# Weights 64 bytes and rests 192 bytes aside, and three groups of 512-column products made in two halves of 256

## The chip, the cores and the metric

The kernel runs on one core of a Trainium2 chip. The metric is the device time of one execution in microseconds; the runs of the kernel before agree within 0.1%.

## The reference

Two layers of a transformer trunk over 512 tokens of width 1024, all in float32, with a final RMS norm. Cut to what matters:

```
for l in range(2):
    h = rmsnorm(x, attn_norm[l])
    sb_q, sb_k, sb_v, df_q, df_k, df_v = split(h @ w_in[l])     # six parts of 512 columns
    sb_out = stick_breaking_attention(sb_q, sb_k, sb_v)         # 8 heads of 64
    df_out = differential_attention(rope(df_q), rope(df_k), df_v, lam)   # 4 heads, two softmaxes each
    df_out = rmsnorm(df_out, subln_norm[l]) * (1 - lambda_init)
    x = x + concat(sb_out, df_out) @ w_o[l]
    h = rmsnorm(x, mlp_norm[l])
    x = x + square(relu(h @ w_ff1[l])) @ w_ff2[l]               # width 4096
return rmsnorm(x, final_norm)
```

## The kernel before, in words

Every float32 operand is split into two parts that TensorE takes as float32r: `hi`, a rounded copy, and `lo`, the rest. A product of two such pairs is three matmuls into the same PSUM bank, in a fixed order: `three` (line 304) issues hi x hi (L310), hi x lo (L311) and lo x hi (L312). I call the three a triple. The first operand of a matmul is stationary (128 columns, loaded into the array ahead of the product, the PEld rows of the profile); the second is the moving one, 512 or 256 columns here. Within a triple the stationary operand is `ah`, `ah`, `al`, the moving one `bh`, `bl`, `bh`, and each matmul has a load of its own, also where the stationary operand stays the same.

Weights come in units of 128 x 1024 floats. A list of units (`_unit_list`, line 51) fixes their order through both layers. The class `_Weights` loads a unit from HBM into one of three raw tiles and splits it (`split_part`, line 120): ScalarE writes `hi` (L118), VectorE subtracts and writes `lo` (L135). The tiles of the split come from pools in rotation; `whi` has 1024 columns, `wlo` has 1152, of which a unit uses 1024 from a starting column that its kind decides: 16 for "s" units, 48 for "v" units, 0 for all others (`NARROW`, line 40). A column is 4 bytes, so 16 columns are 64 bytes and 48 are 192. All the tiles named here begin at multiples of 256 bytes. The first two "w" units of each layer are split into `md_hi` and `md_lo` instead (`W.home`), which have no starting column.

The kinds of units, with what the products are made of:

- "x": projections of the differential attention's queries and keys; weights stationary, 512 tokens of the normed activations `h_hi`, `h_lo` moving. Made by `block` (line 320).
- "p": projections of the stick-breaking attention's queries and keys, 16 units in both layers together, also by `block`; 8 triples of 512 columns each.
- "w": values of the softmax (differential) attention, 4 units a layer, in `all_values` (line 454): activations stationary, 512 columns of weights moving; 8 triples a unit.
- "v": values of the stick-breaking attention, in `values_of`: activations stationary, weights moving in 256 columns, 128 triples in all.
- "o": output projection, in `wo` (line 795): weights stationary, 512 tokens of the attention's output moving. Half 1 (`md_hi`, `md_lo`) runs among the attention's products, half 0 (`ms_hi`, `ms_lo`, which share their tiles with `vd_hi`, `vd_lo`) after them; 64 triples each in both layers.
- "1", "s", "f": the dense stage. "1" units are the first group's products of 512 columns, by `block`. "s" units are the seven forms of a Strassen-like product of the first dense matrix, weights stationary, activations moving in 256 columns: 7 forms x 8 triples x 2 x 3 groups x 2 layers. "f" units are the forms of the second matrix, weights moving in 512 columns.

Products of 256 columns are not read and written in order: `walked` (line 298) cuts the columns into groups of 32 and takes the groups from the last to the first, for the moving operand and the PSUM bank alike. `three` does this when it is given a `step`; products of 512 columns are taken straight.

In the attention stage the order of TensorE's queue is written out by a planner in the code: `dense` yields after each triple (each six, for "v"), with an assumed cost, and pieces of `attn` (scores S, transposes T, sums O) are put between. The page's names for the outputs are `p0s1k` (layer 0, stick-breaking, block 1, keys), `p0u` ("v" units), `p0w` ("w" units), `wo`, and X, V, Y, W, Z for the dense stage's banks.

Of the kernel before, what the change touches and what calls it, by code (L numbers as in the profile page):

```python
# [10 lines left out]
F32R = mybir.dt.float32r  # L11
# [6 lines left out]
P = 128  # L18
# [4 lines left out]
KC = D // P  # L23
# [13 lines left out]
MAN = ()  # L37
APART = (("s", 0, 1), ("s", 3, 0), ("s", 3, 1))
_CTX = {}
NARROW = {"s": 16, "v": 48}  # L40
DLY_R, DLY_D, DLY_S, DLY_Q = 3.5, 10.2, 9.0, 6.0
TAIL, ATT, DENSE, CAP = 6.0, 53.0, 145.0, 0.1
FORMS = ("11", "x3", "x2", "21", "x1", "x4", "22")
# [9 lines left out]
def _unit_list():  # L53
    units = []
    def qk(l, cq, ck, b):
        units.append(("p", l, cq + b * P))
        units.append(("p", l, ck + b * P))

    for l in range(L):
        for item in ORDER:  # L60
            b = int(item[1])
            if item[0] == "d":
                units.append(("x", l, b, 0))
                units.append(("x", l, b, 1))
            elif item[0] == "s":
                qk(l, SBQ, SBK, b)
            elif item[0] == "w":
                units.extend(("w", l, part) for part in range(4))
            else:
                units.extend(("v", l, SBV + b * P, half) for half in range(2))  # L70
        for half in (1, 0):
            for j in range(4):
                units.append(("o", l, half, j))
        for g in range(GROUPS):
            if g == 0:
                units.extend(("1", l, f) for f in range(2 * GP))
            else:
                units.extend(("s", l, g, j, form) for j in range(2) for form in FORMS)
            for form in FORMS2:
                for c in range(GP // 2):  # L80
                    units.append(("f", l, g, form, c))
    return units


_UNITS = _unit_list()
# [9 lines left out]
class _Weights:  # L95
# [24 lines left out]
    def split_part(self, i, a, b):  # L120
        nc = self.nc
        if i not in self.tiles and i in self.home:
            self.tiles[i] = self.home[i]
        if i not in self.tiles:
            k = self.spot(i)
            self.owner[k] = i
            self.turn = k + 1
            at = NARROW.get(_UNITS[i][0], 0)
            hi = self.pools[k // 2].tile([P, 1024], F32R, tag="whi", name=f"whi{i}")
            lo = self.pools[k // 2].tile([P, 1152], F32R, tag="wlo", name=f"wlo{i}")[:, at : at + 1024]  # L130
            self.tiles[i] = (hi, lo)
        hi, lo = self.tiles[i]
        raw = self.first if (i, b) == (0, P) else self.raw[i]
        h = self.round(hi[:, a:b], raw[:, a:b])
        self.last = h, nc.vector.tensor_tensor(  # L135
            out=lo[:, a:b], in0=raw[:, a:b], in1=hi[:, a:b].bitcast(F32), op=ALU.subtract)
# [31 lines left out]
def trunk(ctx, tc, opened, xT, w, w2, w1, gfin, lamv, cos, sin, out):  # L168
# [11 lines left out]
    def bank(tag, name):  # L180
        if tag == "any":
            tag = ("mm", "s", "s", "mm", "s")[turn[0] % 5]
            turn[0] += 1
        ring[0] += tag == "s"
        return ps.tile([P, 512], F32, tag=tag, name=name, bufs=banks[tag])
# [3 lines left out]
    W = _Weights(nc, w, wraw, wspl)  # L189
# [37 lines left out]
    def gcol(which, l, c):  # L227
        i = {"attn": l * 8, "mlp": 16 + l * 8, "final": 32, "sub": 40 + l}[which] + c
        return g_all[:, i : i + 1]
# [21 lines left out]
    def make_h(c, g):  # L251
        a = nc.scalar.activation(h_hi[:, c, :], x[:, c, :], AF.Copy, scale=g)
        return a, nc.vector.scalar_tensor_tensor(
            out=h_lo[:, c, :], in0=x[:, c, :], scalar=g, in1=h_hi[:, c, :].bitcast(F32),
            op0=ALU.mult, op1=ALU.subtract)

    def add_sq(c, first, sqt, eng=nc.gpsimd):
        if first:
            return nc.scalar.activation(ssq, x[:, c, :], AF.Square), None
        sq = sqt("sq")  # L260
        s = nc.scalar.activation(sq, x[:, c, :], AF.Square)
        return s, eng.tensor_tensor(out=ssq, in0=ssq, in1=sq, op=ALU.add)
# [35 lines left out]
    def walked(t, step):  # L298
        return t.rearrange("p (a b) -> p a b", b=step)[:, ::-1, :]
# [4 lines left out]
    def three(pt, a, b, first, last, goes_on=False, step=0):  # L304
        ah, al = a
        bh, bl = b
        if step:
            pt, bh, bl = (walked(e, step) for e in (pt, bh, bl))
        return (
            nc.tensor.matmul(pt, ah, bh, start=first, stop=False, skip_group_check=goes_on),  # L310
            nc.tensor.matmul(pt, ah, bl, start=False, stop=False, skip_group_check=goes_on),  # L311
            nc.tensor.matmul(pt, al, bh, start=False, stop=last, skip_group_check=goes_on))  # L312

    def hpair(c):
        return h_hi[:, c, :], h_lo[:, c, :]

    def wpair(u, c, n=P):
        return u[0][:, c * n : (c + 1) * n], u[1][:, c * n : (c + 1) * n]

    def block(name, tag="mm"):  # L320
        pt = bank(tag, name)
        u = W.next("px" if name[0] == "p" else "1")
        for c in range(KC):
            three(pt, wpair(u, c), hpair(c), c == 0, c == KC - 1)
            yield pt if c == KC - 1 else None

    def constants(a2):
# [18 lines left out]
    for l in range(L):  # L346
        with ExitStack() as actx:
# [49 lines left out]
            first = W.split  # L397
# [56 lines left out]
            def all_values():  # L454
                pts = [bank(tag, f"p{l}w{tb}") for tb, tag in enumerate(("s", "s", "s", "o"))]
                for part in range(4):
                    u = W.next("w")
                    for n in range(2):
                        c = 2 * part + n
                        wide = wpair(u, n, 512)  # L460
                        for tb, pt in enumerate(pts):
                            h = [e[:, c, tb * P : (tb + 1) * P] for e in (h_hi, h_lo)]
                            W.product = three(pt, h, wide, c == 0, c == KC - 1)[2]
                            if c == KC - 1:
                                hi, lo, r = vd_hi[:, tb, :], vd_lo[:, tb, :], rcol[:, tb : tb + 1]
                                nc.scalar.activation(hi, pt, AF.Copy, scale=r)
                                nc.vector.scalar_tensor_tensor(
                                    out=lo, in0=pt, scalar=r, in1=hi.bitcast(F32), op0=ALU.mult, op1=ALU.subtract)
                            yield
                for i in range(4):  # L470
                    ready[("vd", i)] = clock[0] + 2.5
# [323 lines left out]
            def wo(half):  # L795
                for j in range(4):
                    u = W.next("o")
                    for dd in range(2):
                        db = 2 * j + dd
                        pt = bank("mm" if half else "any", f"wo{l}{half}{db}")  # L800
                        for e in range(4):
                            a = u[0][:, e * 256 + dd * P : e * 256 + dd * P + P]
                            b_ = u[1][:, e * 256 + dd * P : e * 256 + dd * P + P]
                            mh, ml = (md_hi, md_lo) if half else (ms_hi, ms_lo)
                            three(pt, (a, b_), (mh[:, e, :], ml[:, e, :]), e == 0, e == 3)
                            if e < 3:
                                yield 3 * 0.216
                        nc.vector.tensor_add(x[:, db, :], x[:, db, :], pt)
                        if half == 0:
                            ends["h"] = make_h(db, gcol("mlp", l, db))  # L810
                            add_sq(db, db == 0, tt, nc.vector)
                        yield 3 * 0.216

            def dense(pts):
# [24 lines left out]
                for item in ORDER[1:]:  # L839
                    kind, b = item[0], int(item[1])  # L840
                    for which in ("qk" if kind in "ds" else "v"):
# [12 lines left out]
                        if kind in "ds":  # L854
                            {"s": evict_s, "d": evict_d}[kind](pt, kind, b, which)
                yield from wo(1)

            at = attn()
            done = 2 * KC * 3 * 0.216 if l else 0.0
            spent = credit = 0.0  # L860
            live = True
            for cost in dense(pts if l else None):
# [5 lines left out]
                while live and credit > 0:  # L868
                    c = next(at, None)
# [17 lines left out]
        with ExitStack() as fctx:  # L887
# [3 lines left out]
            last = l == L - 1  # L891
# [327 lines left out]
            for g in range(GROUPS):  # L1219
# [24 lines left out]
                for form in FORMS2:  # L1244
# [20 lines left out]
                    for n, (c, i, r, part) in enumerate(work):  # L1265
                        if c not in held:
                            held[c] = W.next("f")
                        u = held[c]
                        hi, lo = (e[:, :, i, :] for e in sides[c])
                        rs = slice(r * P, r * P + P)  # L1270
                        mine = [m for m, e in enumerate(work) if e[2:] == (r, part)]
                        pt, b_ = to[r], wpair(u, i, 512)
                        if part:
                            pt = halves[part - 1][:, 0:256]
                            b_ = [e[:, 256 * part - 256 : 256 * part] for e in b_]
# [8 lines left out]
                        if end and not last and form == "22" and n % 2:  # L1284
                            h = back(n // 2)
# [19 lines left out]
                    if end and last and form == "x1":  # L1305
                        done = ((2, 0), (3, 0), (0, 1), (1, 1))
                        squares = [square(*e) for e in done]
                        weighed = [weigh(*e) for e in done]
                    elif end and last and form == "x4":
                        first = [came[0]]  # L1310
# [5 lines left out]
            else:  # L1316
# [6 lines left out]
                for n in range(KC):  # L1323
                    if n in (3, 5):
                        for c_ in (n + 1, n + 2):
                            h = back(c_)
# [81 lines left out]
```

## Time and profile before

| | us |
|---|---|
| median of 3 runs (1111.13 to 1112.01) | 1111.6 |
| the profiled execution | 1111.63 |
| its span, from the first instruction to the last | 1109.9 |
| PE busy (6345 matmuls) | 1102.4 |
| PEld busy | 964.3 |
| DVE busy | 907.7 |
| ACT busy | 688.6 |

Busy times are sums of recorded durations. PE's recorded matmuls overlap, so the time from one product's start to the next product's start, called a step here, is what a product costs. The rows of a group read: line, engine, operation, output and inputs, shape of the moving operand, count, then busy us and mean ns of one.

### The profile page before, as it was taken

Reading aid. Unit: us, or ns where it says so; the run is one execution under the profiler, and the core shown is the slowest. Engines: PE = TensorE matmul, PEld = TensorE weight load, DVE = VectorE, ACT = ScalarE, POOL = GpSimd, SP = SyncE. Lnnn points to the kernel's source line nnn. Section 1 sums busy time; section 2 is a strip of 40 time slices with the busy share of each in tenths; the row PEclk is TensorE's granted clock in tenths of the full one; section 3 lists DMA queues with packets and bytes.
Section 4 is the critical chain, followed back from the end, with each engine's and each line's share of the span. In section 5 each row is a group of like instructions: output and inputs, shape, how many; then the busy total and the mean of one; then the engine's idle time right before and its main releaser. Section 6 shows DMA issues by size and latency. Waiting matters only on the chain.

```text
span 1109.9 us, 17170 instructions
## 1 busy us (share of the span) xinstructions
PE 1102.4 (99%) x6345; PEld 964.3 (87%) x6345; DVE 907.7 (82%) x1333; ACT 688.6 (62%) x1131; POOL 151.9 (14%) x233
## 2 busy tenths in 40 slices
PE   9999999999999999999999999999999999999997
PEld 7889889888899899899878898888888998998986
DVE  7799688798658879779877897887797787797797
ACT  6447777567558458467345576675774484674765
POOL 1001343101011001001000013530010010010010
PEclk9999999999999999999999999999999999999999
DMA  7476343269777788758325654522577877787462
GB/s 244 146 190 190 112 127 107 83 217 229 185 210 176 179 213 184 191 142 214 110 76 146 189 161 131 161 69 76 208 172 179 210 184 175 203 189 200 123 133 96
DMA packets 61044, 181.25 MB, mean 163 GB/s; under 512 B 7456, under 2 KB 8736, under 8 KB 60960
## 3 DMA queue, kind: packets, MB, share of 16 engines
q1 hardware_dynamic: 50160, 141.84, 40.6%
q0 software_dynamic: 10368, 37.75, 19.8%
q8 instruction: 50, 0.82, 0.3%
q10 hardware_dynamic: 432, 0.56, 0.1%
q14 instruction: 34, 0.28, 0.1%
HBM read 150.77 MB, written 4.19 MB: 140 GB/s over the span
## 4 chain that ended last, share of the span: by engine, by line
PE 97%; DVE 1%; issue 1%; ACT 0%; POOL 0%; POOLq 0%; DVEq 0%; ACTq 0%
PE X L311 9%; PE X L312 9%; PE X L310 9%; PE V L311 4%; PE V L312 4%; PE V L310 3%; PE wo L310 3%; PE wo L312 3%; PE wo L311 3%; PE f L312 3%; PE f L310 3%; PE f L311 3%; PE Y L311 2%; PE Y L312 2%; PE Y L310 2%; PE W L310 1%
## 5 line engine op out<-in xcount | busy, mean ns | idle before, releaser
L118 ACT ACTIVATE whi<-q 128x1024 fp32r<-128x1024 f32 x96 | 101.4, 1057 | 103.9 <-PE X L312 38.1
L135 DVE TENSOR_TENSOR wlo<-q,whi 128x1024 fp32r<-128x1024 f32 x96 | 116.8, 1221 | 42.8 <-ACT whi L118 42.6
L135 DVE TENSOR_TENSOR wlo<-raw,whi 128x1024 fp32r<-128x1024 f32 (+1 forms) x82 | 96.7, 1186 | 6.7 <-ACT whi L118 6.4
L118 ACT ACTIVATE whi<-raw 128x1024 fp32r<-128x1024 f32 (+1 forms) x82 | 80.9, 994 | 33.8 <-issue 17.9
L310 PE MATMUL X<-whi,Ah 128*128 128x512 f32 x248 | 97.4, 393 | 0.0
L312 PE MATMUL X<-whi,Al 128*128 128x512 f32 x248 | 96.7, 390 | 0.0
L311 PE MATMUL X<-wlo,Ah 128*128 128x512 f32 x248 | 96.6, 390 | 0.0
L135 DVE TENSOR_TENSOR wlo<-waves,whi 128x1024 fp32r<-128x1024 f32 x40 | 48.8, 1220 | 15.8 <-ACT whi L118 15.6
L118 ACT ACTIVATE whi<-waves 128x1024 fp32r<-128x1024 f32 x40 | 42.2, 1056 | 29.0 <-PE X L312 18.9
L310 PEld LDWEIGHTS X<-whi,Ah 128*128 128x128 f32 x248 | 46.5, 188 | 11.9 <-DVE y L1132 1.9
L312 PEld LDWEIGHTS X<-whi,Al 128*128 128x128 f32 x248 | 46.5, 188 | 9.8
L311 PEld LDWEIGHTS X<-wlo,Ah 128*128 128x128 f32 x248 | 46.6, 188 | 9.0
L311 PE MATMUL X<-h_lo,whi 128*128 128x256 f32 x192 | 53.6, 279 | 0.0
L311 PE MATMUL X<-hxl,whi 128*128 128x256 f32 x192 | 53.6, 279 | 0.0
L312 PE MATMUL X<-h_hi,wlo 128*128 128x256 f32 x192 | 53.2, 277 | 0.0
L312 PE MATMUL X<-hxh,wlo 128*128 128x256 f32 x192 | 53.2, 277 | 0.0
L310 PE MATMUL X<-h_hi,whi 128*128 128x256 f32 x192 | 52.6, 274 | 0.0
L310 PE MATMUL X<-hxh,whi 128*128 128x256 f32 x192 | 52.6, 274 | 0.0
L310 PE MATMUL f<-h_hi,whi 128*128 128x512 f32 x128 | 50.4, 393 | 0.0
L312 PE MATMUL f<-h_hi,wlo 128*128 128x512 f32 x128 | 49.9, 390 | 0.0
L311 PE MATMUL f<-h_lo,whi 128*128 128x512 f32 x128 | 49.8, 389 | 0.0
L242 DVE TENSOR_TENSOR Al<-x,Ah 128x512 fp32r<-128x512 f32 (+1 forms) x60 | 46.5, 791 | 3.6 <-ACT Ah L241 3.5
(764 smaller groups left out, 3686.9 us busy)
## 6 DMA issues: line engine op xcount, KB each, us to landing
raw<-in_w SPq DMA_DIRECT2D x78, 512.0 KB, 3.6
q<-in_w SPq DMA_DIRECT2D x48, 512.0 KB, 4.6
q<-in_w POOLq DMA_DIRECT2D x48, 512.0 KB, 8.4
waves<-in_w SPq DMA_DIRECT2D x28, 512.0 KB, 4.5
first_a<-in_w SPq DMA_DIRECT2D x12, 512.0 KB, 5.0
first_b<-in_w SPq DMA_DIRECT2D x12, 512.0 KB, 5.3
first_c<-in_w SPq DMA_DIRECT2D x12, 512.0 KB, 4.3
first_b<-in_w POOLq DMA_DIRECT2D x12, 512.0 KB, 6.8
```

What stands on the lines that cost most here:

```text
L118: return self.nc.scalar.activation(o, src, AF.Copy)
L135: self.last = h, nc.vector.tensor_tensor(out=lo[:, a:b], in0=raw[:, a:b], in1=hi[:, a:b].bitcast(F32), op=ALU.subtract)
L242: nc.vector.tensor_tensor(out=lo, in0=src, in1=hi.bitcast(F32), op=ALU.subtract)
L310: nc.tensor.matmul(pt, ah, bh, start=first, stop=False, skip_group_check=goes_on),
L311: nc.tensor.matmul(pt, ah, bl, start=False, stop=False, skip_group_check=goes_on),
L312: nc.tensor.matmul(pt, al, bh, start=False, stop=last, skip_group_check=goes_on))
```

## The change

Units of five kinds ("s", "v", "p", "o", "w") get their `hi` from column 16 of its tile (64 bytes) and their `lo` from column 48 (192 bytes); both tiles have 1088 columns. The triples of the "p" units, the "w" units and the output projection are made as two triples of 256 walked columns each, by a new function `three_halves`: first the three products of the left half, then the three of the right half. The "x" and "1" units stay with triples of 512 columns, and so do the "f" units. The planner's costs and the places where `dense` yields are the same.

```diff
-NARROW = {"s": 16, "v": 48}
+NARROW, PLACES, PAD = "svpow", (16, 48), 64
...
-            at = NARROW.get(_UNITS[i][0], 0)
-            hi = self.pools[k // 2].tile([P, 1024], F32R, tag="whi", name=f"whi{i}")
-            lo = self.pools[k // 2].tile([P, 1152], F32R, tag="wlo", name=f"wlo{i}")[:, at : at + 1024]
+            hi, lo = (
+                self.pools[k // 2].tile([P, 1024 + PAD], F32R, tag=f"w{n}", name=f"w{n}{i}")[:, at : at + 1024]
+                for n, at in zip(("hi", "lo"), PLACES if _UNITS[i][0] in NARROW else (0, 0)))
...
+    def three_halves(pt, a, b, first, last):
+        for n in range(2):
+            cols = slice(256 * n, 256 * n + 256)
+            done = three(pt[:, cols], a, [e[:, cols] for e in b], first and n == 0, last and n == 1, True, 32)
+        return done
+
...
     def block(name, tag="mm"):
         pt = bank(tag, name)
+        some = three_halves if _UNITS[W.used][0] == "p" else three
         u = W.next("px" if name[0] == "p" else "1")
         for c in range(KC):
-            three(pt, wpair(u, c), hpair(c), c == 0, c == KC - 1)
+            some(pt, wpair(u, c), hpair(c), c == 0, c == KC - 1)
...
-                            W.product = three(pt, h, wide, c == 0, c == KC - 1)[2]
+                            W.product = three_halves(pt, h, wide, c == 0, c == KC - 1)[2]
...
-                            three(pt, (a, b_), (mh[:, e, :], ml[:, e, :]), e == 0, e == 3)
+                            three_halves(pt, (a, b_), (mh[:, e, :], ml[:, e, :]), e == 0, e == 3)
```

## The prediction

> **What bounds the kernel now.** I read the page's span and chain first, then the waits of TensorE, then the stretches, and then single products in the timeline and the groups of instructions by shape.
>
> ```profile
> span 1109.9 us, 17170 instructions
> ...
> PE 97%; DVE 1%; issue 1%; ACT 0%; POOL 0%; POOLq 0%; DVEq 0%; ACTq 0%
> ```
>
> ```profile
> PE warm L225 <- POOL edge L219: 1.4, 1, 1.4
> ```
>
> ```profile
> 25.00:211.00 186.00, 186.00 (x1054) 161.93 (x1053) 158.78 (x295) 116.04 (x258) 42.21 (x71) 1.00 0.48 136
> 243.00:560.00 317.00, 317.00 (x1904) 281.35 (x1903) 254.30 (x301) 195.07 (x249) 31.89 (x38) 1.00 0.72 185
> ```
>
> TensorE carries 97% of the chain and has one recorded wait in the whole execution (1.4 us at the start). The third view has the stretch, its length, the busy time of PE, PEld, DVE, ACT and POOL, the clock, the DMA share and GB/s: in the attention stage (25 to 211) and in the dense stage (243 to 560) PE is busy for every microsecond, DVE for 85 and 80% of it, and the granted clock is 1.00. So the time is the number of products times the step from one product to the next, and I cost the change in steps alone. The profiled execution took 1111.63 us (span 1109.9, and 1.7 around it); the median of the runs is 1111.6, so the sum is made against 1111.6.
>
> **The step of a product.** A matmul's recorded duration runs on past the start of the next, so steps are read from starts.
>
> ```profile
> 399.83 0.27 PE L310 MATMUL V<-hxh,whi 128*128 128x256 f32 x1
> ...
> 404.69 0.27 PE L310 MATMUL Y<-h_hi,whi 128*128 128x256 f32 x1
> ```
>
> ```profile
> 215.82 0.39 PE L310 MATMUL wo<-vdh,whi 128*128 128x512 f32 x1
> ...
> 218.54 0.39 PE L310 MATMUL wo<-vdh,whi 128*128 128x512 f32 x1
> ```
>
> From 399.83 to 404.69 lie 14 triples (L310, L311, L312) of 256-column products of "s" units: 4.86 us, 347 ns a triple. From 215.82 to 218.54 lie four triples of 512 columns: 2.72 us, 680 ns a triple. Two halves at today's price are thus 694 ns against 680: splitting alone loses 14 ns a triple where nothing disturbs it.
>
> ```profile
> L311 PE MATMUL X<-h_lo,whi 128*128 128x256 f32 x192 | 53.6, 279 | 0.0
> ...
> L312 PE MATMUL X<-h_hi,wlo 128*128 128x256 f32 x192 | 53.2, 277 | 0.0
> ...
> L310 PE MATMUL X<-h_hi,whi 128*128 128x256 f32 x192 | 52.6, 274 | 0.0
> ...
> L310 PE MATMUL wo<-mdh,whi 128*128 128x512 f32 x64 | 26.4, 412 | 0.0
> ...
> L312 PE MATMUL wo<-mdh,wlo 128*128 128x512 f32 x64 | 25.1, 393 | 0.0
> L311 PE MATMUL wo<-mdl,whi 128*128 128x512 f32 x64 | 25.1, 393 | 0.0
> ...
> L310 PE MATMUL wo<-vdh,whi 128*128 128x512 f32 x64 | 24.9, 389 | 0.0
> ...
> L310 PE MATMUL p1w<-mdh,h_hi 128*128 128x512 f32 x16 | 6.4, 407 | 0.0
> L310 PE MATMUL p0w<-whi,h_hi 128*128 128x512 f32 x16 | 6.3, 394 | 0.0
> ...
> L310 PE MATMUL half<-whi,Ah 128*128 128x256 f32 x4 | 1.1, 283 | 0.0
> ```
>
> The means tell the steps apart. The three "s" rows sum to 830, the triple to 347, so a mean is the step plus 161; the 512 row at 389 and the 680 give 389 - 227 = 162. Products of one width, in one loop, then step 113 (274), 118 (279) and 116 (277) ns. What differs between them in the code is which weights are loaded for the next product: L310 is followed by the same `hi`, L311 by `lo`, L312 by the next `hi`. The moving operand is walked in groups of 32 columns from the last group back, so it starts 896 bytes behind its own beginning, which is 128 past a multiple of 256. Taking distances modulo 256, the next weights lie 128 from it behind L310 and L312, and 64 behind L311 (`lo` is 64 bytes aside). The row named half is a 256-column product with no walk and no distance: 283, the dearest that runs undisturbed. So place is worth up to 9 ns of a step (274 to 283), but no row has the new places, and two rows with distance 128 differ by 3 ns, so the step isn't a function of the one distance alone.
>
> **The change part by part.** Call T the time of three undisturbed 256-column products in the new places; today's is 347.
>
> "s" units (84 units of 8 triples, 672): 672 x (T - 347).
>
> "v" units (128 triples), by the groups of a stretch of the attention stage (90 to 115 us):
>
> ```profile
> L310 PE MATMUL p0u<-whi,h_hi 128*128 128x256 f32 x32 | 9.2, 286 | 0.0
> L311 PE MATMUL p0u<-wlo,h_hi 128*128 128x256 f32 x32 | 9.0, 280 | 0.0
> L312 PE MATMUL p0u<-whi,h_lo 128*128 128x256 f32 x32 | 8.9, 279 | 0.0
> ```
>
> They sum to 845, less 483 is 362; as the 161 is known to 1 ns only, I take 360, or 13 over the undisturbed 347 for life between attention's products, and keep the 13: 128 x (T - 347). These products run in sixes, as each new pair of halves will, so a six in this stage costs 2T + 26.
>
> "p" blocks (16 of 8 triples, 128), by the groups of one of them (121 to 130 us):
>
> ```profile
> L310 PE MATMUL p0s1k<-h_hi,whi 128*128 128x512 f32 x8 | 3.2, 404 | 0.0
> L312 PE MATMUL p0s1k<-h_hi,wlo 128*128 128x512 f32 x8 | 3.1, 392 | 0.0
> L311 PE MATMUL p0s1k<-h_lo,whi 128*128 128x512 f32 x8 | 3.1, 391 | 0.0
> ```
>
> 1187 less 3 x 162.3 is 700 a triple. I take 705 for all of them, between this and the 711 of the next part, which runs in the same stage: 128 x (2T + 26 - 705).
>
> Output projection, half 1 (64 triples, inside attention): 412 + 393 + 393 - 487 = 711, so 64 x (2T + 26 - 711). Half 0 (64 triples, after attention, 680): 64 x (2T - 680).
>
> Softmax values, "w" units (64 triples): with 389 for their second and third products, the rows with 407 and 394 first make 698 and 685, and undisturbed it is 680; I take 689. Two of the four units of a layer are split into the tiles of `md_hi` and `md_lo` (the `home` of the weights), which the change doesn't move: 32 x (2T + 26 - 689) for the moved ones and 32 x (720 - 689) for the others.
>
> The sum: at T = 347 the terms are 0, 0, 1.9, 0.6, 0.9, and 1.0 + 1.0 us, together +5.4; each ns of T weighs 672 + 128 + 256 + 128 + 128 + 64 = 1376 times, so the change is 5.4 + 1.376 x (T - 347) us. It breaks even at T = 343.
>
> Other costs I put at nothing. The split's two passes:
>
> ```profile
> L135 DVE TENSOR_TENSOR wlo<-q,whi 128x1024 fp32r<-128x1024 f32 x96 | 116.8, 1221 | 42.8 <-ACT whi L118 42.6
> L135 DVE TENSOR_TENSOR wlo<-first_a,whi 128x1024 fp32r<-128x1024 f32 x24 | 29.4, 1225 | 19.7 <-ACT whi L118 19.2
> ```
>
> Rests of "f" units start at 0 (q) and rests of "s" units 64 bytes aside (first_a); 1221 and 1225 ns say that a write's place doesn't matter. If it did, DVE's spare fifth hides it; without that cover 100 ns on each of some 160 splits would be 16 us. The tiles take 1088 + 1088 columns where they took 1024 + 1152, so no other tile moves, and no DMA, wait or order changes. The 960 more weight loads hide under the products:
>
> ```profile
> 72.29 0.76 PE T0d L661 x7
> ```
>
> Seven 128-column transposes, each with its own load, step 109 ns, so a load needs no more than that and a 256-column product can't be pushed past 109 by it. That is also the floor: T is at least 327. The ceiling is the half row, 3 x 283 - 483 = 366.
>
> Where T falls between 327 and 366 no row says. I take 339, what three products like today's cheapest cost (3 x 274 - 483): in the new places no walk starts at distance 0 or 128 from the next weights any more, every one is 64 to one side or the other, and a layout in which the three lines see the same distances should let the three pay alike, at the price that one of them already has. Against it stands L311, the one line with 64 today and the dearest. So: 672 x -8 = -5.4, 128 x -8 = -1.0, "p" -0.1, half 1 -0.4, half 0 -0.1, "w" +1.5, together -5.6 us, or 1106.0.
>
> A rule speaks against the placing. The Trainium skill, "SBUF — State Buffer", section "Who interferes with whom", gives TensorE two independent read ports, one for the moving operand and one for the weights, and says that it never waits on anyone. By that rule the places would change nothing. The trace agrees with it only in part: the 274, 279 and 283 above are one width with different places. The skill's "TensorE: Matmul & The Clock Gate", section "Back-to-back issue gap", has N/2.4 + 2.5 ns a product, by which 960 more products would cost an estimated 2.4 us; here the steps are 116 and 227 where it has 109 and 216.
>
> **The rivals.** First, places do nothing and T stays 347; then splitting costs its 14 ns in the open and gains nothing among attention's products, since "v" shows that sixes of 256 suffer there as 512s do. That is +5.4 us, 1117.0, slower. For it: the 3 ns between two lines of equal distance, so something besides place sets the step. It decides above T = 343.
>
> Second, 64 bytes is a bad distance, as L311 says: each product pays 279, T = 3 x 279 - 483 = 354, and the change is 5.4 + 9.6 = +15.0, 1126.6. For it: the dearest "s" row has that distance. Against: "v" has its rests at that distance too, and its L311 (280) costs 1 ns more than its L312 (279), not more.
>
> Third, the two effects cancel: T between 341.5 and 344.7 leaves the time within 2.2 us, which is the 0.2% that a measurement of this kernel can tell from no change. A gain that another engine takes back would look the same; DVE at 80% and one wait of PE in the whole execution speak against that.
>
> Fourth, more is gained: T near 333, half of the way from 339 to the floor, makes -13.9, 1097.7.
>
> **How the numbers follow.** T from 335 to 341 gets 0.35 (the forecast, 1106), near 333 and below 0.13, cancelling 0.14, unchanged 347 0.17, the dear 354 and above 0.21. That is 0.48 faster, 0.14 same, 0.38 slower. The range leaves out the least likely ends, below T = 333 and above T = 352: 1097 to 1124. It holds cases of both signs; the forecast's own range is 1100 to 1109.
>
> **What would show it.** TensorE's instructions become 7305. If right, the three lines of the "s" products have one mean near 274, the distances of starts give 339 a triple, wo and p rows appear as 128x256 twice as often with means up to 13 over that in attention and without it behind it, and the s part of the dense stages shortens by some 5.4 us while attention hardly changes. Means of 279 in three lines make the second rival right, 274, 279 and 277 unchanged the first. I am wrong altogether if PE gets waits that it doesn't have now, or if attention's products in halves cost far from 2T + 26, which would show that a disturbed six isn't priced by "v".

## The result, and the profile after

The change took 1126.28 us (1125.9 to 1127.14, four runs) against 1111.37 (1111.04 to 1112.01) for the kernel before: a ratio of 1.0136 with a 95% interval of 1.012 to 1.0151, 14.9 us slower. The forecast was 5.6 us faster; sign and range are both missed. The profiled execution of the change took 1126.45 us.

The page of after: its span, the first engine lines and the chain.

```profile
span 1124.7 us, 19077 instructions
...
PE 1115.8 (99%) x7305; PEld 1018.4 (91%) x7305; DVE 908.0 (81%) x1333; ACT 689.5 (61%) x1131; POOL 153.7 (14%) x233
...
PE 89%; DVE 4%; ACT 2%; POOL 2%; issue 1%; DMA 1%; POOLq 0%; SPq 0%; DVEq 0%; ACTq 0%
```

TensorE has the 7305 matmuls that were foreseen and is still the bound; DVE's busy time is 908.0 as against 907.7. The chain's share of PE fell from 97 to 89%, which looks like a new bound and isn't one. Followed back, the chain of after leaves TensorE between 115 and 165 us and between 672 and 721 us, in the attention of both layers, and runs over pieces of ScalarE, VectorE and GpSimd. In both layers it comes back to TensorE behind a transpose T whose step is 360 and 382 ns, where before has 239 and 223: 0.3 us in both together. In experiment 1 the halves lose more and PE has 98% of the chain, so the share doesn't tell what a change costs. The waits of TensorE in after (line, releaser, us in all, times, longest):

```profile
PE warm L225 <- POOL edge L219: 1.4, 1, 1.4
PE p L827 <- ACT whi L118: 0.4, 1, 0.4
PE p L831 <- ACT h_hi L252: 0.4, 1, 0.4
```

Two waits of 0.4 us are new. Both are in the very first projection, 4 to 9 us after the start, which as a whole is 0.5 us longer; variants of before show such a wait too (0.6 us in experiment 4, 0.3 us in experiment 9). The rest is in the steps. First the groups by shape of after's "s" products:

```profile
L311 PE MATMUL X<-h_lo,whi 128*128 128x256 f32 x192 | 54.3, 283 | 0.0
...
L310 PE MATMUL X<-h_hi,whi 128*128 128x256 f32 x192 | 53.6, 279 | 0.0
...
L312 PE MATMUL X<-h_hi,wlo 128*128 128x256 f32 x192 | 53.5, 278 | 0.0
```

Then two rows of the timeline of after, 14 triples apart:

```profile
404.28 0.28 PE L310 MATMUL X<-h_hi,whi 128*128 128x256 f32 x1
...
409.27 0.28 PE L310 MATMUL X<-hxh,whi 128*128 128x256 f32 x1
```

Means of 283, 279 and 278 where before had 279, 274 and 277; 4.99 us over 14 triples is 356 ns a triple where it was 347. Read closely, the triples alternate between 360 and 353, in all 84 "s" units; their mean is 356.6. So T, on which the sum hung, is 356.6 and not 339.

To see the whole difference I added up, in each trace, the time from every product's start to the next one's, by kind (us):

| kind | before | after | difference |
|---|---|---|---|
| "s" | 233.00 | 239.64 | +6.6 |
| "p" | 90.14 | 92.05 | +1.9 |
| "w" | 44.37 | 46.18 | +1.8 |
| output projection, half 0 | 43.52 | 44.59 | +1.1 |
| output projection, half 1 | 45.55 | 46.44 | +0.9 |
| scores S and sums O between them | 73.70 | 74.87 | +1.2 |
| first projection of layer 0 | 23.68 | 24.22 | +0.5 |
| behind the last product | 6.31 | 6.82 | +0.5 |
| "v", "f", "1" | 440.51 | 440.85 | +0.3 |

One thing in this trace contradicts any account by places alone. Half 0 of the output projection is the same code with the same places in both layers. Its groups in layer 0 (215 to 232 us):

```profile
L311 PE MATMUL wo<-vdl,whi 128*128 128x256 f32 x37 | 10.5, 283 | 0.0
L310 PE MATMUL wo<-vdh,whi 128*128 128x256 f32 x37 | 10.3, 279 | 0.0
L312 PE MATMUL wo<-vdh,wlo 128*128 128x256 f32 x36 | 10.0, 278 | 0.0
```

and in layer 1 (780 to 798 us):

```profile
L312 PE MATMUL wo<-vdh,wlo 128*128 128x256 f32 x51 | 14.1, 276 | 0.0
L310 PE MATMUL wo<-vdh,whi 128*128 128x256 f32 x50 | 13.8, 276 | 0.0
L311 PE MATMUL wo<-vdl,whi 128*128 128x256 f32 x50 | 13.8, 276 | 0.0
```

By the rule that a mean is the step plus 161, the first makes 357 ns a triple and the second 345; from starts it is 356.6 and 340.0. The same products in the same places run at two prices. I call such a settled price a round: a 357 round and a 340 round.

### The profile page after: what moved, and what is told of

Read it like the earlier page. It is cut to its first block, busy times and chain, and to the rows that moved or that the text cites. A ratio compares the mean times of both kernels' runs of the same rounds, so it can differ in the third digit from the quotient of the medians.

```text
span 1124.7 us, 19077 instructions
## 1 busy us (share of the span) xinstructions
PE 1115.8 (99%) x7305; PEld 1018.4 (91%) x7305; DVE 908.0 (81%) x1333; ACT 689.5 (61%) x1131; POOL 153.7 (14%) x233
## 4 chain that ended last, share of the span: by engine, by line
PE 89%; DVE 4%; ACT 2%; POOL 2%; issue 1%; DMA 1%; POOLq 0%; SPq 0%; DVEq 0%; ACTq 0%
PE X L310 9%; PE X L311 9%; PE X L312 9%; PE V L311 4%; PE V L310 4%; PE V L312 3%; PE wo L311 3%; PE wo L310 3%; PE wo L312 3%; PE f L310 3%; PE f L312 3%; PE f L311 3%; PE Y L311 2%; PE Y L310 2%; PE Y L312 2%
## 5 line engine op out<-in xcount | busy, mean ns | idle before, releaser
L135 DVE TENSOR_TENSOR wlo<-raw,whi 128x1024 fp32r<-128x1024 f32 (+1 forms) x82 | 96.5, 1182 | 10.3 <-ACT whi L118 10.0
```

The lines of the kernel that those rows point to most:

```text
L135: self.last = h, nc.vector.tensor_tensor(out=lo[:, a:b], in0=raw[:, a:b], in1=hi[:, a:b].bitcast(F32), op=ALU.subtract)
```

## The experiments

Places are given as hi/lo in bytes, so before has its "s" units at 0/64 and the change at 64/192. "s" per triple is always from starts. Every kernel here computes the whole of the reference. Kernels with a ratio were timed in rounds against the kernel before; the others ran once, and what counts there is the price of single blocks of triples, not the total.

**1. Halves alone.** The change with before's places:

```diff
+            places = (0, {"s": 16, "v": 48}.get(_UNITS[i][0], 0))
```

> The halves of the change with the places of before (rests of s units 64 bytes aside, rests of v units 192, all else 0). Theory 'place' (the new places are what costs most, and the s units alone lose 6.6 us by them): s triples stay at 347 ns, the halves cost what the prediction's sum has at T = 347, +5.4 us at most, so 1115 to 1117. Rival 'split' (places are neutral and the loss comes from 960 more products): most of the 14.9 us, 1123 to 1126, with s triples near 357 again.

Measured: 1121.05, ratio 1.0084 (1.007 to 1.0098), 9.5 us slower. "s" is back at 347 (233.00 us). Its half 0 of the output projection, groups by shape:

```profile
L312 PE MATMUL wo<-vdl,whi 128*128 128x256 f32 x128 | 36.0, 281 | 0.0
L311 PE MATMUL wo<-vdh,whi 128*128 128x256 f32 x128 | 36.0, 281 | 0.0
L313 PE MATMUL wo<-vdh,wlo 128*128 128x256 f32 x128 | 36.0, 281 | 0.0
```

At 0/0 the three products of a half cost 3 x 281 - 483 = 360 by this rule, 356 from starts (45.57 us over 128), not 347. "p" took 93.03 us. The time lies between the two ranges that were expected and in neither. So the halves are dear by themselves, and dearer at 0/0 than at the places of the change.

**2. Places alone.** The change with `three` in the place of `three_halves`:

```diff
-        some = three_halves if _UNITS[W.used][0] == "p" else three
+        some = three
```

and likewise for "w" and the output projection.

> The places of the change in all five kinds of units, and no halves: p, w and output products are 512 columns again. Theory 'place': s triples near 357, alternating 360 and 353, and +6.6 us from them, +0.2 from v; 512-column triples as before: 1118 to 1119. Rival 'split': 1111 to 1112.

Measured: 1120.38, ratio 1.0078 (1.0065 to 1.009), 8.8 us slower. "s" took 239.65 us: the whole of its loss is due to the places. Products of 512 columns don't like the new places either ("p" +0.4, "w" +0.4, half 0 +1.0), which the expected 1118 to 1119 had not counted. The two parts together make 18.3 us, the change 14.9, so they don't add up: where both meet, the new places are better for halves than 0/0 ("p" 92.05 for 93.03, half 0 44.59 for 45.57), and the price that whole products pay for them falls away.

**3 and 4. Which places?** Before, with the place of the "s" units chosen by block (layer, group, half of the columns), twelve places in a kernel:

```diff
+            places = PLACES[u[1] * 6 + (u[2] - 1) * 2 + u[3]] if u[0] == "s" else (0, 48 if u[0] == "v" else 0)
```

> The kernel before with the places of hi and lo of the s units different in each of the 12 blocks of 56 triples (layer, group, half); in order, bytes of hi and lo: 0 0, 64 0, 128 0, 192 0, 0 128, 64 64, 128 128, 192 64, 0 192, 128 64, 192 192, 64 128. Theory 'place': the mean triple differs by block between 333 and 360 ns; equal places (0 0, 64 64, 128 128, 192 192) are alike if only the distance between hi and lo counts, and unlike if the distance to the moving operand counts. Rival 'split': 347 in all. A third theory, 'entry' (with one layout a chain can settle on a fast or a slow round, decided by the time at which it starts): blocks in which the triple is fast in one form and slow in another.

> As the first sweep, with, in order, bytes of hi and lo: 0 64, 128 192, 64 192, 192 128, 0 64, 64 192, 128 192, 0 0, then under 64 bytes: 0 32, 32 0, 32 96, 16 48. Theory 'place': both blocks of 0 64 at 347, both of 64 192 at 357 as in the change, both of 128 192 alike, and 0 0 as in the first sweep. Theory 'entry': a pair with the same places differs. If 64 bytes is the finest step that counts, 16 48 is like 0 0; if not, the last four blocks have times of their own.

Measured, ns a triple in each block, from starts:

| hi/lo | sweep 1 | hi/lo | sweep 2 |
|---|---|---|---|
| 0/0 | 359.9 | 0/64 | 346.8, 346.8 |
| 64/0 | 346.8 | 128/192 | 353.5, 353.5 |
| 128/0 | 357.4 | 64/192 | 356.5, 340.2 |
| 192/0 | 354.5 | 192/128 | 353.4 |
| 0/128 | 354.9 | 0/0 | 355.9 |
| 64/64 | 340.1 | 0/32 | 353.6 |
| 128/128 | 359.9 | 32/0 | 373.0 |
| 192/64 | 340.4 | 32/96 | 359.8 |
| 0/192, 128/64 | 356.1, 353.3 | 16/48 | 355.0 |
| 192/192, 64/128 | 353.3, 353.2 | | |

The triples range from 340 to 373, 11 ns a step, a little more than the 9 that before's rows showed. Each place stands here in one block or two; every second block follows a block at another place, the others follow an "f" unit, so the table gives a place and its neighbour together. And 64/192, the place of the change, appears at both prices in one kernel. The timeline of the second sweep, 32 triples from the first row to the second, and 32 from the third to the fourth:

```profile
402.41 0.28 PE L314 MATMUL X<-hxh,whi 128*128 128x256 f32 x1
...
413.82 0.28 PE L314 MATMUL X<-hxh,whi 128*128 128x256 f32 x1
...
499.70 0.28 PE L314 MATMUL X<-hxh,whi 128*128 128x256 f32 x1
...
510.58 0.28 PE L314 MATMUL X<-hxh,whi 128*128 128x256 f32 x1
```

11.41 us over 32 is 356.6; 10.88 over 32 is 340.0. The dear block follows 512-column products of an "f" unit, the cheap one follows directly on a block at 0/64. That speaks for the theory 'entry', which the next experiments test: a layout allows one or several rounds, and what ran before decides which of them the chain falls into. 0/0 has two prices as well, 359.9 and 355.9. The rival was that 64/64 is simply the better place.

**5 and 6. 64/64 in place of 64/192,** in the change ("s", "p" and "o" units) and, for the "s" units alone, in before:

```diff
-NARROW = {"s": 16, "v": 48}
+PLACES = {"s": (16, 16), "v": (0, 48)}
...
```

> The change with one number different: the rests of s, p and o units 64 bytes aside like their weights, not 192 (v and w units as in the change). Theory 'place': s triples 340 ns in all 12 blocks, so 672 x (340 - 356.6) = -11.2 us against the change by the s units alone, and halves of p and output products nearer to 340 as well: 1111 to 1114, about even with before. Theory 'entry': 64 64 has a slow round too and some blocks fall on it: 1116 to 1124.

> The kernel before with s units at 64 and 64 bytes, nothing else changed and no halves. Theory 'place': 340 in all 12 blocks, -4.5 us, 1107. Theory 'entry': some blocks at 355 to 360, each of 56 triples costing 0.5 to 0.7 us more than at 347: 1107 to 1119.

Measured: 1125.07, ratio 1.0125 (1.0112 to 1.0139), and 1115.91, ratio 1.004 (1.0026 to 1.0054). In both kernels every "s" block ran at 353.3, though the sweep had shown 340.1 at these very places. The first kernel is slower than either range that was expected; the second lies within the range of 'entry', though with all blocks dear and none cheap. Groups of the second:

```profile
L312 PE MATMUL X<-h_lo,whi 128*128 128x256 f32 x192 | 53.8, 280 | 0.0
L311 PE MATMUL X<-h_hi,whi 128*128 128x256 f32 x192 | 53.6, 279 | 0.0
L313 PE MATMUL X<-h_hi,wlo 128*128 128x256 f32 x192 | 53.6, 279 | 0.0
```

At 64/64 all three lines have the very same distance from the walk's start to the next weights, which is what the forecast wanted of its layout, and they still pay 279 and 280. The rival fell. In the sweep 64/64 came right behind a block at 0/128; here it comes behind "f" units or itself.

**7. 192/64** for the "s" units of before, which the sweep had at 340 behind another block:

```diff
+PLACES = {"s": (48, 16), "v": (0, 48)}
...
```

> The kernel before with s units at 192 and 64 bytes. Theory 'place': 340 in all blocks as in the one block of the first sweep, 1107. Theory 'entry': its mirror image, 64 192, was at 340 in one block and at 356.6 in another, so some blocks slow: 1107 to 1118.

Measured: 1106.81, ratio 0.9962 (0.995 to 0.9975), 4.7 us faster. Its groups:

```profile
L312 PE MATMUL X<-h_lo,whi 128*128 128x256 f32 x192 | 53.0, 276 | 0.0
...
L311 PE MATMUL X<-h_hi,whi 128*128 128x256 f32 x192 | 53.0, 276 | 0.0
...
L313 PE MATMUL X<-h_hi,wlo 128*128 128x256 f32 x192 | 53.0, 276 | 0.0
```

One mean in all three lines, 340.1 a triple, in eleven of the twelve blocks of the profiled execution; in the twelfth two single triples of 478 and 460 ns and the two behind them raise the mean to 345, and then the chain is at 340 again. Behind "f" units, behind itself and, in the sweep, behind a block at 360, 192/64 fell into the 340 round: no entry that was tried leads it elsewhere. This version beats both kernels. Its profiled execution is the slowest of the five (1108.42 us) and has a wait that before doesn't have, 0.8 us in the second matrix's products for a rest that VectorE writes; experiments 12 and 14 have one too (0.9 and 0.4 us). With shorter steps, the split begins to come late there.

**8 and 9. The entry itself.** The kernel before, with six of the seven forms at the change's 64/192 and only the first form of each block, "11", elsewhere: at 64/64 in one kernel, at 192/64 in the other, whose line this is.

```diff
+            places = (48, 16) if _UNITS[i][-1] == "11" else PLACES.get(_UNITS[i][0], (0, 0))
```

> The kernel before with s units at 64 and 192 bytes as in the change, but the first of the seven forms of each block (11) at 64 and 64. Theory 'entry': the first form brings the chain into step, and the six forms behind it stay at 340 with the very places that cost 356.6 in the change: 1107. Theory 'place' in its plain form (a layout has one price): 340 in the first form, 356.6 in the other six, 672 x (6/7 x 9.9 - 1/7 x 6.7) = +5.1 us, 1116.6.

> As the entry test before, but the first form of each block lies at 192 and 64 bytes, which was at 340 in all blocks; the six forms behind it at 64 and 192 as in the change. Theory 'entry': they stay at 340, 1107. Theory 'place' in its plain form: 356.6 in six of seven forms, 672 x (6/7 x 9.9 - 1/7 x 6.7) = +5.1 us, 1116.6.

Measured: 1118.01, ratio 1.0059 (1.0047 to 1.0072), and 1106.88, ratio 0.9962 (0.9948 to 0.9976). The first was meant as a fast entry and was none, since 64/64 ran at 353 there itself; beside the second it serves as its counterpart. The timeline of the first, from the second form of a block to the block's end (48 triples, all at 64/192):

```profile
321.60 0.28 PE L311 MATMUL V<-hxh,whi 128*128 128x256 f32 x1
...
338.72 0.28 PE L311 MATMUL X<-h_hi,whi 128*128 128x256 f32 x1
```

and of the second, the same 48:

```profile
321.54 0.28 PE L311 MATMUL V<-hxh,whi 128*128 128x256 f32 x1
...
337.86 0.28 PE L311 MATMUL X<-h_hi,whi 128*128 128x256 f32 x1
```

17.12 us over 48 is 357, 16.32 over 48 is 340. The code and the places of these 48 triples are the same; only the eight triples ahead of them differ. That holds in all 12 blocks of both. So the entry decides, and 64/192 is not dear in itself.

**10. The change at 192/64** for "s", "p" and "o" units:

```diff
+PLACES, PAD = {"s": (48, 16), "p": (48, 16), "o": (48, 16), "v": (16, 48), "w": (16, 48)}, 64
...
```

> The change with weights of s, p and o units at 192 and rests at 64 bytes (v and w units as in the change): the layout that I took T = 339 for does exist, so this tests the rest of the prediction's sum. By it: 5.4 + 1.376 x (340 - 347) = -4.2 us, 1107.2. By what the halves cost in the runs so far (p and half 1 together about +2.8 with s at 347 or 357, w +1.8, their neighbours S and O +1.2): s -4.2, half 0 about 0, the rest +3 to +5.5, so 1110 to 1113.

Measured: 1113.1, ratio 1.0018 (1.0009 to 1.0027), 2.0 us slower. "s" gave 4.4 us back and half 0 of the output projection ran as in before:

```profile
L312 PE MATMUL wo<-vdh,wlo 128*128 128x256 f32 x128 | 35.3, 276 | 0.0
L310 PE MATMUL wo<-vdh,whi 128*128 128x256 f32 x128 | 35.3, 276 | 0.0
L311 PE MATMUL wo<-vdl,whi 128*128 128x256 f32 x128 | 35.3, 276 | 0.0
```

43.53 us over 64 is 680 a pair of triples: two halves of the cheapest round cost what one triple of 512 costs, so the split has nothing to gain even there. The other halves still lose: "w" +1.7, "p" +0.7, half 1 +0.3, the pieces S and O between them +1.0. Transposes (T) +1.0, the first projection and the end +0.5 each and small terms (+0.5) complete the 1.8 by which its profiled execution is longer than that of before.

**11 and 12. Places for the 512-column products** of the "1" units (and "f" units in the first), with "s" at 192/64, straight in the first kernel, in groups of 32 columns from the last in the second:

```diff
+ONES = tuple((16 * (n // 4), 16 * (n % 4)) for n in (0, 5, 10, 15, 1, 4, 2, 8, 3, 12, 6, 9, 7, 13, 11, 14))
...
```

> Before with s at 192 64, and the places of the 512-column products of the dense stage swept: 16 pairs over the 16 units of kind 1, 8 pairs over the 8 groups of f units. If the rounds of 512-column products depend on places too, triples differ from 680 (660 or 700); if 512 columns leave the load time enough, all stay at 680.

> Before with s at 192 64; the products of units of kind 1 are walked in groups of 32 columns, with the same 16 pairs of places. If walking helps 512 columns as it does 256 (360 without, 340 at the best place), some units come to 660; otherwise 680 or more.

Measured, ns a triple once the eight triples of a "1" unit have settled: taken straight, 680 at 0/0 and 687 to 701 at every other place; walked, 680 at 128/128, 696 and 704 by turns at 0/0 and 686 to 702 elsewhere. The groups of the first's second-matrix products, whose "f" units were moved as well:

```profile
L314 PE MATMUL X<-whi,Ah 128*128 128x512 f32 x248 | 98.6, 398 | 0.0
L316 PE MATMUL X<-whi,Al 128*128 128x512 f32 x248 | 97.7, 394 | 0.0
L315 PE MATMUL X<-wlo,Ah 128*128 128x512 f32 x248 | 97.5, 393 | 0.0
```

393, 390 and 390 before. A triple of 512 columns has its 680 already; none of the places that were tried goes below it, which fits experiment 2's small losses. Each place ran behind one neighbour only.

**13 and 14. Distance, or the walk?** One kernel shifts the moving operand and the weights of three forms by the same 64 bytes, which leaves the distances of before; the other takes the 256 columns straight at 64/192, which gives each line the distance that the walked 192/64 gives it.

```diff
-                                  form in ("11", "x3") and pr == c == 0, pr == 1 and c == 3, True, 32)
+                                  form in ("11", "x3") and pr == c == 0, pr == 1 and c == 3, True, 0)
```

> The kernel before, but in three of the seven forms of the s units (x3, x2, 22) the moving operand lies 64 bytes further on and the weights lie at 64 and 128 bytes: all three operands shifted by 64 bytes together. If the distance between moving operand and weights counts: 347 ns a triple there as before. If the place of the weights itself counts: 353, as 64 128 had in the first sweep. The other four forms (0 64): 347.

> The kernel before with s units at 64 and 192 bytes and their 256 columns taken straight instead of walked. Straight, the moving operand starts at 0 modulo 256 instead of 128, so the distances are those that 192 64 has when walked. If only distances modulo 256 count: 340 ns a triple and about 1107. If the walk itself matters (straight products without distance cost 360): 347 or more.

Measured: the second took 1107.86 with 340.0 to 340.4 in all 12 blocks:

```profile
L311 PE MATMUL X<-h_hi,whi 128*128 128x256 f32 x192 | 53.0, 276 | 0.0
L313 PE MATMUL X<-h_hi,wlo 128*128 128x256 f32 x192 | 53.0, 276 | 0.0
L312 PE MATMUL X<-h_lo,whi 128*128 128x256 f32 x192 | 53.0, 276 | 0.0
```

So the walk isn't needed for 340, and distances from the moving operand's start to the next weights account for this pair. The first didn't answer: shifted and unshifted forms alike ran between 348 and 360 (1118.08 in all), the unshifted ones too, which run at 347 among their own kind; in the second block of each group all seven forms took 359 to 360. The two layouts alternate here, so place and entry can't be told apart. Whether a place counts beside the distance is left open.

**15. The change, entered cheaply.** Its own 64/192 everywhere but in the first form of each block:

```diff
+                for n, at in zip(("hi", "lo"), (48, 16) if _UNITS[i][-1] == "11" else PLACES if _UNITS[i][0] in NARROW else (0, 0)))
```

> The change with one of seven forms of the s units (11, the first of each block) at 192 and 64 bytes, all else as in the change. Theory 'entry': all seven forms at 340, so 672 x (340 - 356.6) = -11.2 us against the change, 1115.1; halves as in the change, still 3.5 us or more slower than before. Theory 'place' in its plain form: only the first form gains, 1124.7.

Measured: 1116.51, ratio 1.0043 (1.0028 to 1.0057). "s" fell to 340.1 (228.57 us), 11.1 less than in the change, with six of seven forms where the change has them. The whole is 9.8 below the change. What is missing of the 11.1 is mostly in half 0 of the output projection, +1.1, which now ran in the dear round in both layers; its groups over both:

```profile
L311 PE MATMUL wo<-vdl,whi 128*128 128x256 f32 x128 | 36.2, 283 | 0.0
L310 PE MATMUL wo<-vdh,whi 128*128 128x256 f32 x128 | 35.7, 279 | 0.0
L312 PE MATMUL wo<-vdh,wlo 128*128 128x256 f32 x128 | 35.7, 279 | 0.0
```

Here 45.66 us, 44.59 in the change, 43.52 in before. Its layer 1 lost the 340 round, though neither its places nor the products straight ahead of it were edited: the last edited product ran some 270 us earlier. What ran just before is thus not all that decides. This rests on one profiled execution of each kernel.

## Why the prediction was wrong

**What bounds the kernel** held: TensorE's steps are the time, 7305 products, and no write place shows a cost (DVE 908.0). The only new waits on record, the two of 0.4 us, lie ahead of every changed unit.

**The step that failed** is the choice of T = 339: "a layout in which the three lines see the same distances should let the three pay alike, at the price that one of them already has". T was 356.6, so the "s" term 672 x (T - 347) came out at +6.6 for -5.4: 12.0 of the 20.3 us by which the forecast missed. The distances were worked out rightly, and experiments 9 and 15 show that these very places can run at 340, the price that was forecast. What the step left out is that a price is not a function of the layout: the layout of the change has a 340 and a 357 round, and from the "f" units it enters the dear one. Nothing in before's rows could show that: each layout stands there with one price. Reading a price per line (274 for one distance, 279 for another) was the mistake below it. The three steps of a triple belong to one repeating pattern; 64/64, where the three lines are alike, ran at 353 or 340 as a whole.

**The halves.** "2T + 26" for a six in attention was wrong in its slope. With T = 356.6 it makes 739; "p" measured 92.05 us over 128, 719, next to the formula's 720 at T = 347; at 192/64, with T = 340, it measured 709 where the formula has 706, and at 0/0 727. The "v" term, 128 x (T - 347), makes +1.2, and "v" measured +0.2. With the T that was measured the whole sum makes +18.6, and the change took 14.9: the size of T was not the only fault. In attention the pattern is broken up by other products every few triples, so a price of the settled chain carries over only in part (that this is the cause is argued, not shown). The units that aren't "s" cost +5.8 us together, by coincidence near the +5.4 that the sum had at T = 347, and far from the -0.1 that it had at T = 339: another 5.9 of the miss.

**What wasn't costed:** the scores and sums between the halves (+1.2), the first projection and the end (+0.5 each), "f" (+0.2): 2.4, which completes the 20.3. Of the 1.2, about 0.9 lies in single long steps: 16 of them are more than 40 ns over the usual step of their width, and 4 in before. They look like waits too short for the view of waits; that they are is not shown.

**The second rival** gave 1126.6, within 0.4 us of the result, by luck: by a mechanism that the runs refute. It had 64 bytes as a bad distance, for which each product pays 279; in experiments 7, 9, 14 and 15 every product starts 64 to one side of the next weights, and the three pay 276, or 113 ns a step. Its parts don't fit either: it made 4.7 of "s" and 10.3 of the rest, measured are 6.6, 5.8 and 2.4 that it didn't know. A time that agrees is no proof of its cause.

**The first rival** had one half of the truth: splitting brings nothing by itself. Experiment 10 sharpens it: 2 x 340 is 680.

**Left open:** what makes a round. That moving operand and weight load get in each other's way on their reads is suggested by distance modulo 256 (experiment 14), not shown. The place of the "s" units, with nothing else edited, moved their triple from 340.1 (experiment 7) to 353.3 (experiment 6). The Trainium skill, "SBUF — State Buffer", section "Who interferes with whom", gives TensorE two independent read ports and knows contention only on the pair that VectorE and GpSimd share; no run here shows a port. Why "f" units lead 64/192 into 357 and 192/64 into 340 wasn't settled, nor whether it is the places of the products ahead or the moment at which they end that sets the entry. The floor that the prediction took, T = 327, was not reached: no settled block is below 340.

## What to carry to other kernels

Here the step of a product with a weight load of its own depended on where the operands lie and on what ran before, by up to 11 ns of 113 at 256 columns and 7 of 227 at 512. If a kernel is bound by such steps, sweep places inside one kernel, then run the best one alone, behind its real neighbours, and prefer the place that falls into its cheap round from every entry; 64/64 was at 340 in the sweep and at 353 alone. Read such prices from starts over many products, and compare the same code at two points of one trace before giving a price to a line. Two halves of a product need a cheaper column to be worth it; here the best halves only matched the whole.

## What the runs showed of the hardware that was not expected

- The same instructions in the same places have more than one settled price: 340.0 or 356.6 ns a triple at 64/192, 340.1 or 353.3 at 64/64. For 64/192 the eight triples ahead decide it (experiments 8 and 9), and the chain stays in its round for the 48 triples of a block.
- Blocks that repeat one time come near multiples of 6.7 ns: 340.0, 346.8, 353.3, 360 (359.9), 373 (373.0); triples of 512 columns at 680, 687, 693, 700. Other blocks repeat a pattern of several times, with means between (355.0, 357.4).
- An offset below 64 bytes counts as well: 32/0 is the dearest of all places tried (373.0), where 0/0 took 359.9 and 355.9. For 16/48 (355.0) and 0/32 (353.6), in one block each, it is not shown.
- An edit in one stage changed the price in another that it doesn't touch: half 0 of the output projection, layer 1, at 340 in the change and 357 when only the first form of the "s" blocks was moved (one profiled execution of each).
